# First layer: rotations from their angles, chunk matrices from four lags, another order of scans, factors and attention; 448 bytes of gap in the second feed-forward part

## The chip, the cores and the metric

The kernel runs on one core of one Trainium2 chip. The metric is the device time of one execution in microseconds, taken as the median of several runs. The engines are named as in the profile: PE (matrix products; PEld is its weight load), DVE (vector), ACT (activation functions), POOL (GpSimd) and SP, whose queue issues most of the DMAs.

## What is computed

Two blocks on a sequence of 256 tokens of width 1024, all in float32. The first block has two layers; the second block is a mixer, an attention on a memory and a mixture of 32 experts. The change is almost wholly in the first half of the first layer, which is this (cut):

```python
hn = rmsnorm(x, even_norm)
q, k, v, u = split(hn @ even_w_in)             # 512, 128, 128, 512 wide
o_attn = swa_sink_attention(rmsnorm(q), rmsnorm(k), v, sinks)   # 8 heads, window 128
# s5: 32 groups of 16 channels, 64 complex states each
lam = exp(a_re*dt) * (cos(a_im*dt) + i sin(a_im*dt))
w = (lam - 1) / a                              # complex
bu = einsum(u, w * b)
h[t] = lam * h[t-1] + bu[t]                    # scan over 256 steps
y = gelu(re(h) @ c_re - im(h) @ c_im + d * u)
o_ssm = y * sigmoid(y @ w_glu + b_glu)
x = x + concat(o_attn, o_ssm) @ even_w_out
x = x + (silu(rmsnorm(x) @ w_gate) * (rmsnorm(x) @ w_up)) @ w_down
```

The second layer has stick-breaking attention in place of the mixer above, and a feed-forward part of the same shape as the first one.

## The kernel before

The stages run one after the other: `even` (the first half of the first layer), `ffn` 0, `odd`, `ffn` 1, `mixer`, `mem`, `moe`. Weights come in 1 MB pieces through SP's queue. Each engine's instructions are put in order ahead of time from the program's order: an instruction takes its turn by its place in the program, and one whose inputs are not there yet lets later ones go ahead. `self.after(ins)` holds the instructions of its block behind `ins` where they are on the same engine. At run time each engine keeps the order that came out.

`even` (L379) does the state space part and the windowed attention beside each other.

- **Start.** The input, the parameters of the state space part, and the weights of `u` are loaded. `load_b` (L1817) loads the matrices b in eight DMAs of 32 KB through POOL's queue, in runs of 64 bytes; `load_rest` (L1825) loads d and c through SP's. `zeros` (L1804) clears `Q`, the two `bd` tiles and `KT`.
- **`scalars`** (L1859) makes, for 16 columns at a time, the powers of lam (`lam`), the factors `w` and `pw[0..4]` (lam to the i times w) and, by repeated squaring (`square`, L1855), the rotations `E[0..5]` of 4, 8, ... steps.
- **`factors`** (L1984) transposes c on PE. **`inputs`** (L1937) writes b times powers of lam into the `bd` tiles on DVE; **`inputs_T`** (L1945) transposes them on PE into `F`; **`shuffle`** (L2037) brings `u` into the order of four steps a column, on PE, as `U` and `Ud`.
- **`rotations`** (L1957) doubles a table `T` of 64 cosines and sines for each of 16 columns, from the `E`, in six steps of three DVE operations. **`decays`** (L1977) makes the magnitudes `D0`.
- The three products for q, k and v (`qkv`, two halves each) follow on PE; before the fourth half stands `states_in(0)`, whose result `v` the first scan reads.
- **`scan(j)`** (L2061), j from 0 to 3, is seven DVE operations: turn by `T`, two scans, turn back. **`outputs`** (L2003), held behind scan 0, writes c times `pw[i]` into `Q` on DVE for i from 0 to 4. **`direct`** (L2020) makes from `bd` and `Q` the matrices `KT` that act inside four steps: 128 small products on PE in four PSUM tiles, and 16 copies by ACT. **`reads(j)`** (L2085) are the products that give y.
- **Attention.** `qk_norm` (L555) norms k on DVE and transposes q and k on PE. `swa` (L590) goes through `soft_exp` (L618): scores on PE, mask and maximum on DVE, exponentials on ACT; then `transpose_p` (L658) and the product with v (`swo`).
- The order in the program is: rotations, decays, scan 0, outputs, direct, reads 0, qk_norm, the scores and exponentials of both halves, scan 1, reads 1, the rest of the attention, scans and reads 2 and 3, `gate` (L2100: gelu, the gate's product `glu`), and `out_proj`, whose products `acc` with `mixa` (attention) and `mixb` (state space) end the part.

In `ffn` (L268) a loop over 11 column pieces does 96 products `gu` and then 24 products `acc` for the piece before. `gap` puts unused bytes ahead of the pool of `s`, `hh` and `hl`: 448 in the first one and 320 in the second.

Of the kernel before, what the change touches and what calls it, by code (L numbers as in the profile page):

```python
# [17 lines left out]
P = 128  # L18
# [26 lines left out]
class K:  # L45
# [215 lines left out]
    def ffn(self, x, i):  # L261
# [117 lines left out]
    def even(self, x):  # L379
# [35 lines left out]
        V.tensor_copy(gc, pg[:, 0:8])  # L415
        s5.load_b()
        tu.append(self.load_cols(w, 1024))
# [38 lines left out]
        for j in range(3):  # L456
            pq = self.pa("qkv")
            wt = self.load_cols(w, j * 256)
            for t in range(2):
                if 2 * j + t == 3:  # L460

                    s5.states_in(0)
                    first = self.lastmm
                for k in range(8):
                    with self.after(*([first] if 2 * j + t >= 3 else [])):
                        self.mm(pq[:, t * 256:(t + 1) * 256], xT[:, k, t * P:(t + 1) * P], wt[:, k], k == 0, k == 7)
# [36 lines left out]
        for j in range(2, 4):  # L503
            wt = h().bitcast(F32).rearrange("p (a b) -> p a b", a=2)
            nc.sync.dma_start(wt, wo[j * 256:(j + 1) * 256, :].rearrange("(k p) n -> p k n", p=P))
            wos.append(wt)
        s5.reads(0)
# [5 lines left out]
        nc.gpsimd.memset(kT, 0.0)  # L513
# [43 lines left out]
    def qk_norm(self, pool, qk, qg, qT, kT, rq):  # L557
# [12 lines left out]
        for t in range(2):  # L570
# [3 lines left out]
        nc.vector.tensor_copy(rq.rearrange("p t (g h) -> p t g h", g=2),  # L574
                              r[:, :, 0:8].rearrange("p t (h g) -> p t g h", g=2))
# [14 lines left out]
    def swa(self, pool, t, qT, kT, v, sink8, rq, mix):  # L590
# [5 lines left out]
        def score(o, h):  # L596
            self.mm(o, qT[:, h // 2, ts], kT[:, h // 4, h % 2, 0:nk], True, True)

        att, den = self.soft_exp(pool, self.r8("att"), 8, nk, score, lambda h: self.band[:, 256 - nk:], 0.125,
                                 sink8, rq)  # L600
        yield
        pT = self.transpose_p(pool, self.r8("attT"), att, den, 8, nk)
# [12 lines left out]
    def soft_exp(self, pool, s, nh, nk, score, bias, scale, sink8, rq=None):  # L615
# [31 lines left out]
        for h in range(nh):  # L647
            nc.scalar.activation(s[:, h], src[h], AF.Exp, bias=nm[:, h:h + 1], scale=sc[h],
                                 accum_out=den[:, h:h + 1])
# [1134 lines left out]
class S5:  # L1784
# [19 lines left out]
    def zeros(self):  # L1804
        k, G = self.k, self.nc.gpsimd
        self.T = self.fp.tile([P, 2, 16, 64], F32, name="T")
        self.Q = self.fp.tile([P, 2, 16, 5, 32], F32, name="Q")
        G.memset(self.Q.rearrange("p c s k q -> p (c s k q)"), 0.0)
# [7 lines left out]
    def load_b(self):  # L1816
        nc, a = self.nc, self.k.a  # L1817
        self.bn = self.r0[:, 1024:1536].rearrange("p (c s q) -> p c s q", c=2, s=16)
        for c, n in enumerate(("ssm_b_im", "ssm_b_re")):
            for j in range(4):  # L1820
                nc.gpsimd.dma_start(self.bn[:, c, 4 * j:4 * j + 4],
                                    bass.AP(tensor=a[n].tensor, offset=a[n].offset + 2048 * j,
                                            ap=[[16, P], [8192, 4], [1, 16]]))
# [30 lines left out]

    def square(self, out, y):  # L1855
        self.cmul(out, y, y, 2)
        self.nc.vector.tensor_scalar(out[:, 2], out[:, 0], -1.0, None, op0=OP.mult)

    def scalars(self):  # L1859
# [33 lines left out]
        V.scalar_tensor_tensor(lam[1][:, 2:4], e[:, 0:2], -1.0, mb, op0=OP.mult, op1=OP.mult)  # L1893

# [17 lines left out]
        self.cmul(lam[2], lam[1], lam[1], 3)  # L1912
        self.cmul(lam[3], lam[1], lam[2], 3)
        self.mag4 = sm("mag4")
        V.tensor_tensor(self.mag4, mag, mag, op=OP.mult)
        V.tensor_tensor(self.mag4, self.mag4, self.mag4, op=OP.mult)
        e2 = cx("e2")
        self.E = [cx(f"E{i}") for i in range(6)]
        self.square(e2, e)
        self.square(self.E[0], e2)  # L1920
        for i in range(5):
            self.square(self.E[i + 1], self.E[i])
# [34 lines left out]
    def rotations(self, steps):  # L1957

        nc, k, sp = self.nc, self.k, self.sp
        V = nc.vector  # L1960
        T = self.T
        if 0 in steps:
            V.memset(T[:, 0, :, 0:1], 0.0)
            V.memset(T[:, 1, :, 0:1], 1.0)
            self.tb = k.r8("tb").rearrange("p (i m) -> p i m", i=2)
        tb = self.tb
        for i in steps:
            n = 1 << i
            shp = [P, 2, 16, n]
            t1, t2 = [tb[:, i, 0:32 * n].rearrange("p (c s a) -> p c s a", c=2, s=16) for i in range(2)]  # L1970
            V.tensor_tensor(t1, T[:, 1:2, :, 0:n].to_broadcast(shp),
                            self.E[i][:, 0:2, :, None].to_broadcast(shp), op=OP.mult)
            V.tensor_tensor(t2, T[:, 0:1, :, 0:n].to_broadcast(shp),
                            self.E[i][:, 1:3, :, None].to_broadcast(shp), op=OP.mult)
            V.tensor_tensor(T[:, :, :, n:2 * n], t1, t2, op=OP.add)

# [26 lines left out]
    def outputs(self):  # L2003
# [6 lines left out]
        for i in range(5):  # L2010
# [4 lines left out]
            for g in range(2):  # L2015
                pr = slice(64 * g, 64 * g + 64)
                qs = slice(16 * g, 16 * g + 16)
                V.tensor_tensor(Q[pr, :, :, i, qs], v1[pr], v2[pr], op=OP.add)

    def direct(self):  # L2020

        nc, k, Q, KT = self.nc, self.k, self.Q, self.KT
# [142 lines left out]
```

## Time and profile before

| | us |
|---|---|
| median of 3 runs (lowest, highest) | 1346.37 (1346.29, 1349.23) |
| the profiled execution, whole | 1346.77 |
| its span, first to last instruction | 1345.1 |
| PE busy in the span | 1230.3 |
| DVE busy in the span | 647.6 |
| ACT busy in the span | 485.6 |
| POOL busy in the span | 48.3 |

The page's shares are means over stages that have different limits. `even` is the first tenth of the span, so the page's slices tell little of it; the views that do are the chain of waits, the timeline and the table by stretches, each read for that stretch alone.

### The profile page before, as it was taken

The numbers are of one execution on the slowest core, as the hardware profiler recorded it, in microseconds if no ns is written. First come the engines' busy times: TensorE is split into PE (matmuls) and PEld (weight loads), VectorE is DVE, ScalarE is ACT, GpSimd is POOL, SyncE is SP. The second block draws the span as 40 slices with busy tenths as digits, with TensorE's granted clock in tenths as the row PEclk, the third lists the DMA queues.
The fourth block names the chain that finished last, engine by engine and source line by source line (L and its number), as shares of the span: only waits on it lengthen the run. The fifth ranks groups of instructions, "written<-read, shape, count | busy, mean of one in ns | idle before, by whom it ended". The sixth has DMA issues, their size and how long they took to land.

```text
span 1345.1 us, 20184 instructions
## 1 busy us (share of the span) xinstructions
PE 1230.3 (91%) x8427; PEld 909.6 (68%) x8427; DVE 647.6 (48%) x1137; ACT 485.6 (36%) x784; POOL 48.3 (4%) x72
## 2 busy tenths in 40 slices
PE   8899999999999999999999999999778777887786
PEld 7776899998998999998999998964122212222111
DVE  9955866666589766666777587431000101000001
ACT  3264644444577644444556555440000000000002
POOL 4010000001000000000300000000000000000000
PEclk9989999999999999999999999999989999889988
DMA  9401965644434865533562758789999999999996
GB/s 259 115 7 47 350 197 197 197 136 130 141 126 157 288 223 190 191 129 125 169 191 92 251 202 299 287 325 421 421 421 421 421 421 421 421 421 421 421 390 239
DMA packets 143436, 345.79 MB, mean 257 GB/s; under 512 B 9863, under 2 KB 100063, under 8 KB 120302
## 3 DMA queue, kind: packets, MB, share of 16 engines
q1 hardware_dynamic: 141418, 339.40, 68.4%
q0 software_dynamic: 1888, 5.06, 1.3%
q8 instruction: 67, 1.10, 0.3%
q14 instruction: 27, 0.22, 0.0%
q10 hardware_dynamic: 36, 0.01, 0.0%
HBM read 343.38 MB, written 1.06 MB: 256 GB/s over the span
## 4 chain that ended last, share of the span: by engine, by line
PE 58%; DMA 29%; DVE 8%; ACT 3%; issue 1%; SPq 0%; DVEq 0%; ACTq 0%
PE gu L77 20%; PE acc L77 15%; DMA w<-in_w_exp_down_dram 10%; DMA w<-in_w_exp_up_dram 8%; DMA w<-in_w_exp_gate_dram 7%; PE z L77 4%; PE qk L77 2%; PE y L77 2%; PE v L77 2%; PE prj L77 2%; PE mqk L77 2%; DMA b<-in_w_exp_gate_dram 1%; DMA b<-in_w_exp_up_dram 1%; DVE wh L182 1%; PE psT L1718 1%
## 5 line engine op out<-in xcount | busy, mean ns | idle before, releaser
L182 DVE TENSOR_TENSOR wh<-w,wh 128x1024 fp32r<-128x1024 f32 x229 | 276.1, 1223 | 133.0 <-ACT wh L181 132.2
L181 ACT ACTIVATE wh<-w 128x1024 fp32r<-128x1024 f32 x229 | 237.0, 1055 | 188.0 <-PE gu L77 64.7
L77 PE MATMUL gu<-fxh,wh 128*128 128x256 f32 x1408 | 246.9, 278 | 0.7 <-ACT fxh L181 0.7
L77 PE MATMUL gu<-w,xe 128*32 128x512 f32 x920 | 175.9, 663 | 52.3 <-DMA w<-in_w_exp_gate_dram 28.3
L77 PEld LDWEIGHTS gu<-fxh,wh 128*128 128x128 f32 x1408 | 214.5, 188 | 1.8 <-ACT fxh L181 0.9
L77 PE MATMUL gu<-fxl,wh 128*128 128x256 f32 x704 | 195.4, 278 | 0.0
L77 PEld LDWEIGHTS gu<-w,xe 128*32 128x32 f32 x920 | 39.1, 119 | 169.6 <-issue 66.5
L77 PEld LDWEIGHTS gu<-fxl,wh 128*128 128x128 f32 x704 | 133.0, 189 | 0.9
L77 PE MATMUL y<-w,hT 128*32 128x512 f32 x456 | 103.4, 612 | 18.6 <-DMA w<-in_w_exp_down_dram 13.1
L77 PE MATMUL acc<-wh,hh 128*128 128x512 f32 x352 | 110.1, 394 | 0.0
L77 PEld LDWEIGHTS y<-w,hT 128*32 128x32 f32 x456 | 24.5, 110 | 89.7 <-DMA w<-in_w_exp_down_dram 41.7
L77 PEld LDWEIGHTS acc<-wh,hh 128*128 128x128 f32 x352 | 64.4, 188 | 13.4
L77 PE MATMUL acc<-wh,hl 128*128 128x512 f32 x176 | 69.5, 395 | 0.0
L1417 DVE COPY ot<-owT 128x256 f32<-128x256 f32 x8 | 3.4, 428 | 135.7 <-PE owT L1415 135.7
L1459 DVE TENSOR_TENSOR y<-y,gu 128x512 f32<-128x512 f32 x8 | 8.1, 1016 | 113.2 <-PE gu L77 103.4
L1456 ACT ACTIVATE y<-gu 128x512 f32<-128x512 f32 x8 | 4.8, 598 | 149.2 <-PE gu L77 149.2
L1490 DVE COPY y<-y 128x512 f32<-128x512 f32 x7 | 4.8, 692 | 106.1 <-PE y L77 106.1
L1476 ACT ACTIVATE hT<-hT 128x512 f32<-128x512 f32 x8 | 4.8, 597 | 139.5 <-PE hT L1474 139.5
L77 PE MATMUL qk<-oxh,wh 128*128 128x256 f32 x256 | 48.7, 285 | 0.0
L1488 ACT ACTIVATE y<-y 128x512 f32<-128x512 f32 x9 | 5.4, 597 | 114.8 <-PE y L77 114.8
L77 PE MATMUL z<-mxh,wh 128*128 128x256 f32 x256 | 46.6, 281 | 0.0
L77 PE MATMUL gu<-b,xe 128*32 128x512 f32 x104 | 34.7, 611 | 7.1 <-DMA b<-in_w_exp_gate_dram 4.2
(539 smaller groups left out, 2046.1 us busy)
## 6 DMA issues: line engine op xcount, KB each, us to landing
w<-in_w_exp_gate_dram SPq DMA_DIRECT2D x57, 1024.0 KB, 19.8
w<-in_w_exp_up_dram SPq DMA_DIRECT2D x54, 1024.0 KB, 19.8
w<-in_w_exp_down_dram SPq DMA_DIRECT2D x51, 1024.0 KB, 19.8
w<-in_ffn_w_gate_dram SPq DMA_DIRECT2D x22, 1024.0 KB, 5.5
w<-in_ffn_w_up_dram SPq DMA_DIRECT2D x22, 1024.0 KB, 6.8
w<-in_ffn_w_down_dram SPq DMA_DIRECT2D x22, 1024.0 KB, 4.9
w<-in_w_in_dram SPq DMA_DIRECT2D x20, 1024.0 KB, 6.0
w<-in_odd_w_in_dram SPq DMA_DIRECT2D x12, 1024.0 KB, 6.2
```

What stands on the lines that cost most here:

```text
L77: self.lastmm = self.nc.tensor.matmul(out, lhsT, rhs, start=start, stop=stop, **kw).ins
L181: return (self.nc.scalar.activation(h, src, AF.Copy).ins, (eng or self.nc.vector).tensor_tensor(l, src, h.bitcast(F32), op=OP.subtract).ins)
L182: (eng or self.nc.vector).tensor_tensor(l, src, h.bitcast(F32), op=OP.subtract).ins)
L1417: V.tensor_copy(ot, ps[:, 0:256].rearrange("p (t n) -> p t n", t=2))
L1456: nc.scalar.activation(s, hs[0], AF.Silu)
L1459: V.tensor_tensor(sk, s.rearrange(turn, k=4), hs[1].rearrange(turn, k=4), op=OP.mult)
L1476: nc.scalar.activation(hT, ps.rearrange("p (f n) -> p f n", f=4), AF.Copy)
L1488: nc.scalar.activation(y[:, h], yps[h], AF.Copy)
L1490: V.tensor_copy(y[:, h], yps[h])
L1718: k.turned = k.nc.tensor.transpose(ps[:, i * P:(i + 1) * P], xg[:, t, (4 * c + i) * P:(4 * c + i + 1) * P], k.ident).ins
```

## The change

In `even` and its helpers:

- `load_b` issues its eight DMAs from SP, behind the 1 MB piece of `u`'s weights and ahead of `load_rest`.
- `scalars` ends with `lam` and `mag4`. The factors `w` and `pw` go into a new function `holds`, called behind scan 0 and ahead of `outputs`. The repeated squares are gone.
- `rotations` makes the whole table at once: the angle times 4, 8, ... from a constant row, a reduction to one turn in six DVE operations on 1024 columns, and sine and cosine by ACT.
- `inputs_T` stands ahead of `shuffle`; rotations and decays stand right behind it. `states_in(0)` stands before the third half of the q, k, v products in place of the fourth.
- `direct` makes each of its 16 blocks once (32 products, one PSUM tile) and copies it to four places.
- Behind `outputs` come: qk_norm (its DVE part behind the last `Q`), scan 1 (behind the norm), the scores and exponentials, direct, reads 0, scan 2, reads 1, the rest of the attention (its ACT part behind the last exponential), scan 3, reads 2 and 3. The first half's scores use the tile of the turned input in place of one of the four work tiles. The gelus stand behind the last exponential. `kT` is cleared by ACT, where POOL did it.

In the second `ffn` the gap is 448 bytes.

```diff
-            self.gap((448, 320)[i], ctx)
+            self.gap(448, ctx)
...
+        tu.append(self.load_cols(w, 1024))
         s5.load_b()
-        tu.append(self.load_cols(w, 1024))
         s5.load_rest()
...
+        s5.inputs_T()
         s5.shuffle(uT)
-        s5.inputs_T()
+        s5.rotations()
+        s5.decays()
...
-                if 2 * j + t == 3:
+                if 2 * j + t == 2:
                     s5.states_in(0)
...
-        s5.rotations(range(6))
-        s5.decays()
         s5.scan(0)
         with self.after(s5.last):
+            s5.holds()
             s5.outputs()
-        s5.direct()
...
-        s5.reads(0)
...
-        self.qk_norm(ap, qk, qg[:, 0], qT, kT, rq)
+        with self.after(s5.lastq):
+            self.qk_norm(ap, qk, qg[:, 0], qT, kT, rq)
+        with self.after(self.normed):
+            s5.scan(1)
...
         next(swa[0])
         next(swa[1])
-        for j in range(1, 4):
-            s5.scan(j)
+        scored = self.lastmm
+        s5.direct()
...
+        with self.after(scored):
+            s5.reads(0)
+        s5.scan(2)
+        s5.reads(1)
+        with self.after(self.exped):
+            for part in swa:
+                next(part, None)
+        s5.scan(3)
+        for j in range(2, 4):
             s5.reads(j)
-            if j == 1:
-                for part in swa:
-                    next(part, None)
...
-                nc.gpsimd.dma_start(self.bn[:, c, 4 * j:4 * j + 4],
+                nc.sync.dma_start(self.bn[:, c, 4 * j:4 * j + 4],
...
+        V.tensor_tensor(g, self.th[:, :, None].to_broadcast([P, 16, 64]),
+                        self.four[:, None].to_broadcast([P, 16, 64]), op=OP.mult)
+        V.tensor_scalar(n, g, 1.0 / (2.0 * math.pi), magic, op0=OP.mult, op1=OP.add)
+        V.tensor_scalar(n, n, -magic, None, op0=OP.add)
+        for t in (TWO_PI_1, TWO_PI_2, TWO_PI_3):
+            V.scalar_tensor_tensor(g, n, -t, g, op0=OP.mult, op1=OP.add)
+        V.tensor_scalar(g, g, 3.141592, -3.141592, op0=OP.min, op1=OP.max)
+        nc.scalar.activation(self.T[:, 0], g, AF.Sin)
+        nc.scalar.activation(n, g, AF.Abs)
+        nc.scalar.activation(self.T[:, 1], n, AF.Sin, bias=self.quarter, scale=-1.0)
...
+            for c in range(2):
+                for g in range(4):
+                    s = 4 * g + i
+                    k.mm(pk[32 * g:32 * g + 32, i], self.bd[c][:, s, 3], Q[:, c, s, 0:4, :], c == 0, c == 1,
+                         tile_position=(0, 32 * g))
```

## Rows read from the trace of the kernel before

**Rows 1.** Chain that ended last, first 140 us; columns start, us, what:
```profile
44.80 1.75 PE v L77 x16
46.57 1.24 DVE abgh L2072
...
64.16 9.96 PE s5K L77 x144
...
91.90 4.78 ACT att L648 x16
...
97.21 1.98 PE swo L77 x4
```

**Rows 2.** Stretches: us, busy of PE PEld DVE ACT POOL, PEclk, DMA share, GB/s:
```profile
7.68:46.57 38.89, 35.00 (x210) 29.06 (x209) 35.16 (x136) 13.16 (x30) 6.99 (x11) 1.00 0.78 214
97.21:101.00 3.79, 3.79 (x13) 2.00 (x14) 3.79 (x4) 3.07 (x5) 0.00 (x0) 0.55 0.02 4
97.21:133.62 36.41, 36.41 (x172) 22.50 (x173) 21.50 (x31) 16.75 (x24) 0.58 (x1) 0.95 0.14 44
```

**Rows 3.** DVE's groups by shape, 7.4 to 46.6 us (busy, mean ns):
```profile
L1975 DVE TENSOR_TENSOR T<-tb 128x1024 f32<-128x1024 f32 x1 | 1.2, 1224 | 0.0
L1981 DVE COPY D<-mag 128x1024 f32<-128x1024 f32 x1 | 0.7, 680 | 0.0
L1853 DVE TENSOR_TENSOR pw<-cm,cm 128x48 f32<-128x48 f32 x4 | 0.8, 202 | 0.0
```

**Rows 4.** Timeline to 60 us (start, us, engine, line; in brackets idle before, releaser):
```profile
10.20 4.72 SPq L1834 DMA_DIRECT2D params<-in_ssm_c_im_dram  x2
13.88 0.68 DVE L1981 COPY D<-mag 128x1024 f32<-128x1024 f32 x1
18.05 0.42 ACT L1941 ACTIVATE wh<-params 64x256 f32<-64x256 f32 x1 [1.09 <-DMA params<-in_ssm_b_re_dram]
25.95 5.34 PE L77 MATMUL qkv<-w,ex 128*128 128x256 f32 x24
33.66 1.93 PE L77 MATMUL U<-uT,ident 128*32 128x256 f32 x32 [2.36 <-DVE uT L449]
35.52 4.09 PE L1953 MATMUL s5F<-ident,wh 128*128 128x128 f32 x32
50.95 1.06 ACT L566 ACTIVATE qT<-qk 128x1024 f32<-128x1024 f32 x1
51.75 0.68 DVE L2011 TENSOR_TENSOR ub<-cd,w 128x512 f32<-128x512 f32 x1
```

**Rows 5.** Timeline, 65 to 97 us, around the norm and the exponentials:
```profile
65.45 1.39 DVE L2018 TENSOR_TENSOR Q<-ub 64x512 f32<-64x512 f32 x2
...
69.39 0.17 DVE L574 COPY rq<-qr 128x16 f32<-128x16 f32 x1
...
77.30 0.66 PE L77 MATMUL kT<-ident,qk 128*64 128x128 f32 x8
...
80.36 0.29 DVE L633 CUSTOM_DVE_ANT_0 att<-sc,band 128x128 f32<-128x128 f32 x1 [10.59 <-PE sc L77]
...
82.79 0.49 ACT L648 ACTIVATE att<-att,nm,rqs 128x128 f32<-128x128 f32 x1 [1.35 <-DVE nm L645]
```

**Rows 6.** ACT's groups by shape, 82 to 97.3 us:
```profile
L648 ACT ACTIVATE att<-att,nm,rqs 128x256 f32<-128x256 f32 x8 | 4.7, 586 | 0.5 <-DVE att L665 0.5
L648 ACT ACTIVATE att<-att,nm,rqs 128x128 f32<-128x128 f32 x8 | 3.8, 480 | 1.4 <-DVE nm L645 1.4
```

**Rows 7.** Table by stretches, single pieces of the first and second feed-forward part:
```profile
161.10:178.00 16.90, 16.90 (x122) 15.84 (x122) 11.96 (x18) 9.86 (x16) 0.00 (x0) 1.00 0.87 298
178.00:194.40 16.40, 16.40 (x123) 15.42 (x122) 10.17 (x12) 7.59 (x11) 0.00 (x0) 1.00 0.58 193
481.09:497.58 16.49, 16.49 (x122) 15.41 (x122) 10.17 (x12) 7.59 (x11) 0.00 (x0) 1.00 0.73 246
497.58:514.49 16.91, 16.91 (x122) 15.82 (x122) 10.17 (x12) 7.59 (x11) 0.00 (x0) 1.00 0.58 187
```

More of the change, by code (lines that the diff above doesn't have):

```diff
@@ L464, in even @@
                 for k in range(8):
-                    with self.after(*([first] if 2 * j + t >= 3 else [])):
+                    with self.after(*([first] if 2 * j + t >= 2 else [])):
                         self.mm(pq[:, t * 256:(t + 1) * 256], xT[:, k, t * P:(t + 1) * P], wt[:, k], k == 0, k == 7)
@@ L527, in even @@
         next(swa[1])
-        for j in range(1, 4):
-            s5.scan(j)
+        scored = self.lastmm
+        s5.direct()
+        for j in range(2, 4):
+            wt = h().bitcast(F32).rearrange("p (a b) -> p a b", a=2)
+            nc.sync.dma_start(wt, wo[j * 256:(j + 1) * 256, :].rearrange("(k p) n -> p k n", p=P))
+            wos.append(wt)
+        with self.after(scored):
[6 more added lines that the diff above has]
+        s5.scan(3)
+        for j in range(2, 4):
             s5.reads(j)
-            if j == 1:
-                for part in swa:
-                    next(part, None)
         fctx.close()
@@ L1807, in zeros @@
         self.Q = self.fp.tile([P, 2, 16, 5, 32], F32, name="Q")
+        self.four = self.fp.tile([P, 64], F32, name="four")
+        G.iota(self.four, pattern=[[4, 64]], base=0, channel_multiplier=0, allow_small_or_imprecise_dtypes=True)
+        self.quarter = self.fp.tile([P, 1], F32, name="quarter")
+        self.nc.vector.memset(self.quarter, math.pi / 2)
         G.memset(self.Q.rearrange("p c s k q -> p (c s k q)"), 0.0)
@@ L1893, in scalars, with holds @@
         V.scalar_tensor_tensor(lam[1][:, 2:4], e[:, 0:2], -1.0, mb, op0=OP.mult, op1=OP.mult)
+        self.cmul(lam[2], lam[1], lam[1], 3)
+        self.cmul(lam[3], lam[1], lam[2], 3)
+        self.mag4 = sm("mag4")
+        V.tensor_tensor(self.mag4, mag, mag, op=OP.mult)
+        V.tensor_tensor(self.mag4, self.mag4, self.mag4, op=OP.mult)
+        self.th, self.pr3 = th, pr3
+    def holds(self):
+        V, sm, cx = self.nc.vector, self.sm, self.cx
+        lam, pr3 = self.lam, self.pr3
         den, t1, t2, t3 = sm("den"), cx("t1", 2), cx("t2", 2), cx("t3")
@@ L1911, in scalars @@
             self.cmul(self.pw[i + 1], lam[1], self.pw[i], 3)
[L1912 to L1922, printed above, removed]
     def inputs(self):
@@ L1955, in inputs_T, with rotations @@
                 nc.scalar.activation(F[:, c, 4 * j:4 * j + 4], ps.rearrange("p (t n) -> p t n", t=4), AF.Copy)
-    def rotations(self, steps):
-        nc, k, sp = self.nc, self.k, self.sp
+    def rotations(self):
+        nc, k = self.nc, self.k
         V = nc.vector
[L1961 to L1975, printed above, removed]
+        tb = k.r8("tb").rearrange("p (i s a) -> p i s a", i=2, s=16)
+        g, n = tb[:, 0], tb[:, 1]
+        magic = 12582912.0
+        V.tensor_tensor(g, self.th[:, :, None].to_broadcast([P, 16, 64]),
[8 more added lines that the diff above has]
+        nc.scalar.activation(self.T[:, 1], n, AF.Sin, bias=self.quarter, scale=-1.0)
     def decays(self):
@@ L2017, in outputs @@
                 qs = slice(16 * g, 16 * g + 16)
[L2018 removed]
+                self.lastq = V.tensor_tensor(Q[pr, :, :, i, qs], v1[pr], v2[pr], op=OP.add).ins
     def direct(self):
         nc, k, Q, KT = self.nc, self.k, self.Q, self.KT
[L2023 to L2032 removed]
+        ps = k.ps("s5K")
+        pk = ps.rearrange("p (s b q) -> p s b q", s=4, b=4)
+        for i in range(4):
+            for c in range(2):
[3 more added lines that the diff above has]
+                         tile_position=(0, 32 * g))
+        for g in range(4):
             for b in range(4):
[L2034 to L2035 removed]
+                nc.scalar.activation(KT[32 * b:32 * b + 32, 4 * g:4 * g + 4, b:4], pk[32 * g:32 * g + 32, :, 0:4 - b],
+                                     AF.Copy)
     def shuffle(self, uT):
@@ L2105, in gate @@
         yg = self.work().rearrange("p (j t a) -> p j t a", j=4, t=4)
-        for i in range(2):
-            nc.scalar.activation(yg[:, 2 * i:2 * i + 2], self.ys[i], AF.Gelu_apprx_tanh)
+        with k.after(k.exped):
+            for i in range(2):
+                nc.scalar.activation(yg[:, 2 * i:2 * i + 2], self.ys[i], AF.Gelu_apprx_tanh)
         yt = [k.ps("yt"), k.ps("yt")]
```

40 lines of the change are left out of this document (11 added, 29 removed).

## The prediction

> **What bounds the kernel now.** I read the page first, to see which engine is busy where, and then left its means aside: the change lies in the first 140 of 1345 us. There I read the chain of waits from its end backwards, and at each change of engine the timeline beside it. The reader should see four links.
>
> (a) Scan 0 starts at 46.57, when PE delivers its input v [rows 1]. v itself waits behind 48 instructions of q, k, v products (24 of them at 25.95, as many right ahead of v) and behind U and s5F, of which U started only when DVE had uT [rows 1, 4]. DVE is busy 35.16 of the 38.89 us up to there, so it is the engine that made uT and the T late [rows 2]. (b) Behind scan 0 DVE makes Q, and the s5K products on PE wait for it until 64.16, hold PE for 10 us, and k's transposes and the scores stand behind them: DVE sat 10.59 us before the first scores at 80.36, although the norm was done at 69.39 [rows 1, 5]. (c) The exponentials start at 82.79 and end at 91.90 + 4.78 = 96.68 [rows 1, 5]. Their own work is 8 times 0.48 and 8 times 0.586, 8.5 us [rows 6]; the other 5.3 us ACT spent behind a copy of turned probabilities that stands ahead of the second eight in its order and itself waits for DVE [rows 1, 6]. (d) From 97.21 PE has no hole until the products with mixb, 36.41 of 36.41 us [rows 2]. From there on the rest of the kernel hangs on this PE time, so what moves 97.21 moves the end by as much.
>
> **The change part by part, up to scan 0.** DVE loses the 23 steps of holds, the 28 steps of the squares, and the 18 of the doubling. The small steps take 0.2 us each by themselves, and about half of that where the next one doesn't wait for them [rows 3]; I take 0.15 for holds and 0.125 for the squares, which interleave with large operations: 3.5 and 3.5 us (bounds 2.3 to 4.6 and 2.8 to 5.6). The doubling has three operations each of 1024 columns (1.224 us) and of 512, 256, 128, 64, 32 columns; by halves above a floor of 0.2 they make 9.2 us. Added are seven operations on 1024 columns. The product with the angle and the three combined ones I put at the row of T, 1.22; the three with a constant lie between that and the copy of D0, 0.68 [rows 3], and I take the copy, the nearest in form: 4.9 + 2.0 = 6.9 us (bounds 4.8, all seven at the copy's price, to 8.6). In sum DVE has 9.3 us less to do (bounds 5.7 to 14.6), and its 35.16 busy us from 7.68 on [rows 2] would, without a wait, end at 42.8 before and 33.5 now; T's last DVE step, with some 1.5 of waits, near 35. ACT's sine, absolute value and sine follow, three passes of 1024 columns at 1.06 [rows 4], so T is there near 38, 41.6 at the worst bound. No row shows a sine of 1024 columns; a pass of the same columns is the nearest.
>
> PE then decides. From 25.95 it has 32 instructions of q, k, v (5.34/24 each: 7.1), s5F (4.1), U (1.9), v (1.75), 14.9 us in any order [rows 1, 4]; the order of inputs_T and shuffle costs nothing as both must come before v. With a few tenths for the R product that gives v at 41.2 and scan 0 at 41.3, 5.3 us ahead. Of that, 3.5 come from the 16 q, k, v instructions that now stand behind v, and the rest from the wait for uT, 2.36. Bounds: 39.5 if u's products end sooner, 43.5 if PE waits for bd or c once more.
>
> The b matrices now go through SP. They landed at 18.05 from POOL [rows 4], and POOL's clearing of Q no longer stands ahead of their issue. But SP's queue has its own waits: its issue of c already took 4.72 us for two pieces while it waited for earlier loads [rows 4], and now eight pieces stand ahead of d, c and the q, k, v weights. I take b at 16.5 to 18 and c some 2 to 3 us later. Later c is covered by u's second half, which PE can do first; if PE's order puts c's transposes ahead, u and all behind slips by up to 2 us, which is the upper bound above. The Trainium skill ("DMA: Bandwidth & Descriptors", Issuing engines are not separate DMA queues) speaks against this edit: DMAs from any engine share the same 16 DMA engines, and another issuer saves only issue time. By that b would land at 18 as before; the sum would not gain from it, and the start of scan 0 would move by nothing, since PE decides it.
>
> **From scan 0 to the exponentials.** Scan 0 took 5.2 (46.57 to 51.75) [rows 1, 4]: end 46.5. holds, now exposed on DVE: 3.5, to 50. Q five times, each two products of 0.68 that overlap to 1.2 and a pair of 1.39 [rows 4, 5], 2.65: 13.3, to 63.3. The norm, all behind it: a reduction of 1024 columns 1.2, one of 256 0.4, eighteen small steps 3.6, the copy 0.17: 5.4, normed at 68.7 against 69.56. So the attention gains little up to here; holds and the norm in one line have eaten the 5.3. Scan 1 stands next on DVE, 5.2, to 73.9. Meanwhile PE makes k's transposes and the scores, which took 3.1 from the first transpose at 77.30 to the first mask at 80.36 [rows 5]: there by 71.8, behind scan 1. Scores to exponentials took 82.79 - 80.36 = 2.4 [rows 5]: exponentials start at 76.3, 6.5 ahead. What is removed here is s5K's 10 us on the path: the new direct has a quarter of the products (2.5 us on PE, ready when Q's fourth step is done near 60.7) and lies in PE's hole; its 16 copies of some 0.43 lie in ACT's, before 76.3. Were that cover gone, they would cost up to 2.5 + 6.8.
>
> With the attention's ACT part behind the last exponential, the sixteen run without a hole: 8.5 + 0.2, end at 85.0 against 96.68. Two copies of 0.6 and swo starts at 86.9 against 97.21: **10.3 us**. Scan 2 and 3 on DVE (10.4, next to 3.8 of normalisation, from 79 on) end by 95, and PE has swo, transposes, reads 2 and the products with mixa until then. So PE's 36.4 us run through again, and the end of the part moves by 10.3. Bounds: 5 (scan 0 at 43.5, DVE's order letting scan 2 in between the scores, holds at 4.6) to 14 (scan 0 at 39.5; and swo not at half clock: the granted clock from 97.21 to 101 was 0.55, mostly the lower level, 1.2 of 2.4 GHz, so these 3.8 us would shrink by some 1.7 [rows 2] if PE is at the upper level by then).
>
> The clearing of kT on ACT (about 1 us early, ACT idle) and the tile for the first scores cost nothing.
>
> **The gap.** Pieces of the two feed-forward parts have the same instructions, the same busy times of the other engines and a granted clock of 1.00, but take 16.40 in the first (gap 448) from its third piece on, and by turns 16.91 and 16.49 in the second (gap 320): from 464 to 615 us five and four of them. The first one's second piece took 16.90 too [rows 7]. So the pace has at least two values, not from the clock, and the gap is the only difference in the code. If 448 brings the second part to what the first one shows, four pieces gain 0.51 and four 0.09: **2.4 us**. If the pace hangs on something else, it is 0, or a loss of 1.7 when the four of 16.49 take 16.91 too. I take 2.4, by the row that has the same gap.
>
> **Sum.** 1346.77 (the profiled execution, 0.4 above the median) - 10.3 - 2.4 = 1334.1; against the median 1333.7.
>
> **Rivals.**
> A. The gap does nothing; the pace is set elsewhere. For it: a piece at 16.90 under gap 448 [rows 7]. Time 1346.4 - 10.3 = 1336.1.
> B. Half the gain: long operations of the new rotations fill each small pause on DVE between the steps that lead to lam, so that bd comes late, PE waits, and scan 0 starts at 44; and scan 2 slips in ahead of the second half's scores. The D0 copy, late in the program, stood at 13.88 as such a filler [rows 4]. 1346.4 - 5 - (0 to 2.4) = 1339.0 to 1341.4.
> C. Slower: T comes last. In the program rotations stand behind inputs, uT and shuffle. If b lands at 28 because its 64-byte runs and the waits of SP's queue hold it up, inputs (8.7 us) end at 37, uT and Ud at 41, and the 6.9 to 8.6 follow without overlap, to 49; the three ACT passes fall among F's eight copies, and T is there at 55 to 57. Everything behind scan 0 is 45.6 us long as above, so the change loses from a scan 0 at 51.6 on, 1 us for each us: at 57 it is 1351.8. Against it: b landed at 18 by the slower way, and T's angles need only the first steps of scalars, so nothing but order keeps T from starting.
> D. The pace tips in the first feed-forward part, as its second value shows up under gap 448 too [rows 7]: eight pieces by 0.51, 4.1 lost: 1337.8.
>
> **Chances.** Forecast 0.42, A 0.28, B 0.16, C 0.05, D 0.09. A measurement of this kernel tells 0.3%, 4 us, from no change: faster means below 1342.3. Forecast, A, D and most of B lie there, with their spreads: 0.86; same 0.10 (the rest of B, D's far end, the milder half of C); slower 0.04. The range leaves 2 in 10 out: from 1329 (14 in place of 10.3, 2.4, and a pace that tips the good way for a piece or two) to 1341 (B).
>
> **What would show it.** Scan 0's first operation near 41; T's second sine before 40; the last Q near 63 and the norm's copy near 69; the first exponential near 76 and sixteen without a hole; swo near 87, and no hole in PE from there; pieces of 16.40 in the second feed-forward part. Wrong it would be if scan 0 stays at 46, if ACT's copies of KT stand among the exponentials, or if PE shows holes behind 87.

## The result, and the profile after

The changed kernel takes 1332.92 us (median of 4 runs, 1331.50 to 1335.14). The kernel before, run beside it, took 1347.53 us (4 runs, 1346.29 to 1349.23). The ratio is 0.9892, with a 95% interval from 0.9873 to 0.9912: 14.6 us faster, 11.9 to 17.1 by the interval. The forecast was 1333.7 us in a range from 1329 to 1341. The profiled execution took 1333.31 us with a span of 1331.6, 13.5 us less than the span of before.

The chain that ended last, in the changed kernel (start us, us, what), beside [rows 1]:

```profile
31.21 6.67 PE qkv L77 x30
37.88 1.75 PE v L77 x16
39.72 1.24 DVE abgh L2081
...
66.18 1.12 PE kT L77 x8
...
83.10 4.79 ACT att L658 x16
...
89.05 1.08 PE swo L77 x4
```

s5K, 10 us of the chain in [rows 1], is gone from it. Between scan 0 and k's transposes the whole chain is DVE's (scan 0, holds, Q, then the norm), where before it changed to PE.

The table by stretches of the changed kernel (us, busy us and count of PE, PEld, DVE, ACT, POOL, then granted clock, DMA share, GB/s), beside [rows 2] and [rows 7]:

```profile
7.64:39.72 32.08, 32.04 (x201) 26.98 (x200) 25.01 (x75) 16.37 (x33) 0.00 (x0) 1.00 0.83 236
66.18:75.75 9.57, 9.57 (x53) 8.16 (x54) 9.18 (x40) 6.94 (x18) 0.00 (x0) 0.72 0.00 1
89.05:120.36 31.31, 31.31 (x147) 18.29 (x147) 16.19 (x23) 16.37 (x24) 0.57 (x1) 1.00 0.15 51
136.54:149.42 12.88, 12.88 (x100) 12.83 (x99) 10.71 (x17) 8.92 (x10) 0.00 (x0) 0.87 1.06 364
485.79:502.19 16.40, 16.40 (x122) 15.41 (x122) 10.17 (x12) 7.59 (x11) 0.00 (x0) 1.00 0.60 193
502.19:518.59 16.40, 16.40 (x122) 15.41 (x122) 10.17 (x12) 7.59 (x11) 0.00 (x0) 1.00 0.58 193
```

Up to scan 0, PE is now busy 32.04 of 32.08 us and DVE 25.01: the two have changed places as the limit. The last two lines are pieces of the second feed-forward part at one pace.

The timeline of the changed kernel (start, us, engine, line; in brackets idle before, releaser), beside [rows 4] and [rows 5]:

```profile
14.04 0.84 ACT L1952 ACTIVATE wh<-params 64x256 f32<-64x256 f32 x2 [0.66 <-DMA params<-in_ssm_b_im_dram]
15.78 0.84 ACT L1952 ACTIVATE wh<-params 64x256 f32<-64x256 f32 x2 [0.90 <-DMA params<-in_ssm_b_re_dram]
...
19.76 0.63 PE L2000 MATMUL s5C<-ident,params 128*128 128x128 f32 x4
...
38.15 1.15 ACT L1984 ACTIVATE T<-tb,quarter 128x1024 f32<-128x1024 f32 x1
...
58.57 1.96 PE L77 MATMUL s5K<-Q,wh 128*32 128x128 f32 x64 [1.18 <-DVE Q L2027]
...
66.15 0.17 DVE L583 COPY rq<-qr 128x16 f32<-128x16 f32 x1
...
77.01 1.22 DVE L2081 TENSOR_TENSOR abgh<-v,T 128x1024 f32<-128x1024 f32 x1
...
79.74 0.17 DVE L655 TENSOR_SCALAR nm<-m 128x8 f32<-128x8 f32 x1
...
82.28 0.78 DVE L675 TENSOR_TENSOR att<-att,den 128x512 f32<-128x512 f32 x1
...
83.10 0.60 ACT L658 ACTIVATE att<-att,nm,rqs 128x256 f32<-128x256 f32 x1 [2.75 <-DVE att L675]
```

The milestones side by side (starts in us of the span unless it says end; the forecast's last four are before less the moves that it summed):

| | before | forecast | after | moved by |
|---|---|---|---|---|
| scan 0 | 46.57 | 41.3 | 39.72 | 6.85 |
| last Q, end | 66.84 | 63.3 | 61.2 | 5.6 |
| norm's copy | 69.39 | 68.5 | 66.15 | 3.2 |
| first exponential | 82.79 | 76.3 | 74.07 | 8.7 |
| last exponential, end | 96.68 | 85.0 | 87.89 | 8.8 |
| swo | 97.21 | 86.9 | 89.05 | 8.2 |
| products with mixb | 133.62 | 123.3 | 120.36 | 13.3 |
| second piece of the first feed-forward part | 161.10 | 150.8 | 149.42 | 11.7 |
| eleventh piece of the second one | 614.69 | 602.0 | 600.59 | 14.1 |
| end of span | 1345.1 | 1332.4 | 1331.6 | 13.5 |

Few rows moved as planned. Up to the first exponential each came earlier than forecast (scan 0 by 1.6 us, the last Q by 2.1, the first exponential by 2.2); the last exponential's end came 2.9 later and swo 2.1 later; the products with mixb came 2.9 earlier. The next two sections are about these, the gap, and which edit brought what.

### The profile page after: what moved, and what is told of

The parts are those of the page before. It is cut to its first block, busy times and chain, and to the rows that moved or that the text cites. A ratio compares the mean times of both kernels' runs of the same rounds, so it can differ in the third digit from the quotient of the medians.

```text
span 1331.6 us, 19755 instructions
## 1 busy us (share of the span) xinstructions
PE 1221.8 (92%) x8235; PEld 902.4 (68%) x8235; DVE 640.7 (48%) x1097; ACT 489.4 (37%) x788; POOL 40.6 (3%) x64
## 3 DMA queue, kind: packets, MB, share of 16 engines
HBM read 343.38 MB, written 1.06 MB: 259 GB/s over the span
## 4 chain that ended last, share of the span: by engine, by line
PE 59%; DMA 30%; DVE 6%; ACT 4%; issue 1%; SPq 0%; DVEq 0%; ACTq 0%
PE gu L77 20%; PE acc L77 14%; DMA w<-in_w_exp_gate_dram 9%; DMA w<-in_w_exp_down_dram 9%; DMA w<-in_w_exp_up_dram 7%; PE z L77 4%; PE qk L77 2%; PE v L77 2%; PE prj L77 2%; PE mqk L77 2%; PE y L77 1%; DMA b<-in_w_exp_up_dram 1%; DMA b<-in_w_exp_gate_dram 1%; DVE wh L182 1%; PE u L77 1%; PE psT L1728 1%
## 5 line engine op out<-in xcount | busy, mean ns | idle before, releaser
L77 PE MATMUL gu<-b,xe 128*32 128x512 f32 x104 | 41.1, 732 | 7.0 <-DMA b<-in_w_exp_gate_dram 4.2
L77 PE MATMUL z<-mxh,wh 128*128 128x256 f32 x256 | 46.6, 281 | 0.0
```

Source lines behind the costliest of these rows:

```text
L77: self.lastmm = self.nc.tensor.matmul(out, lhsT, rhs, start=start, stop=stop, **kw).ins
```

## Experiments

| kernel | median us | before beside it | ratio, 95% interval | span profiled |
|---|---|---|---|---|
| changed kernel | 1332.92 | 1347.53 | 0.9892 (0.9873, 0.9912) | 1331.6 |
| e1, gap 320 in the second part | 1336.58 | 1348.23 | 0.9916 (0.9898, 0.9933) | 1333.5 |
| e2, gaps swapped | 1334.40 | 1348.23 | 0.9903 (0.9882, 0.9925) | 1332.0 |
| e3, den twice | 1331.89 | 1348.23 | 0.9877 (0.9861, 0.9894) | 1330.1 |
| e4, norm early | 1333.64 | 1348.23 | 0.9881 (0.9863, 0.9899) | 1332.3 |
| u1, old direct | 1332.60 | 1349.06 | 0.9874 (0.9858, 0.9891) | 1330.8 |
| u2, v ahead of the fourth half | 1339.10 | 1349.06 | 0.9925 (0.9908, 0.9941) | 1337.0 |
| u3, b from POOL | 1335.56 | 1348.44 | 0.9897 (0.9881, 0.9914) | 1336.9 |
| b1, before with den twice | 1346.05 | 1348.44 | 0.9989 (0.9977, 1.0001) | 1343.3 |
| b2, before with the rotations | 1353.64 | 1348.44 | 1.0042 (1.0025, 1.0059) | 1350.3 |
| b3, before with v early | 1345.65 | 1348.44 | 0.9973 (0.9963, 0.9983) | 1344.8 |
| c1, den twice, holds early | 1328.72 | 1349.06 | 0.9850 (0.9834, 0.9867) | 1325.3 |
| c2, and outputs early | 1326.78 | 1349.06 | 0.9842 (0.9823, 0.9861) | 1323.8 |

Kernels timed on different chips are compared by their ratios (0.1% is 1.35 us), and a step inside a kernel by its trace: the intervals are some 2.5 us wide to either side, so steps of 2 us are read from the traces. By the ratios alone, e1 to e4, u1 and u3 are not told apart from the changed kernel, u2 is slower than it (by 0.0033, where the two intervals' half-widths combine to 0.0025), and c1 and c2 are faster.

### The gap: e1 and e2

```diff
-            self.gap(448, ctx)
+            self.gap((448, 320)[i], ctx)      # e1
+            self.gap((320, 448)[i], ctx)      # e2
```

> The changed kernel with the second feed-forward part's gap back at 320 bytes; every engine's order is the same. Theory: the gap alone sets the pace of that part's pieces, so they alternate again between 16.91 and 16.49 us where the changed kernel has 16.40, and the ten pieces' starts from the second to the eleventh span 150.5 us in place of 148.1: the kernel loses 2.4 us. Rival: the pace comes from what ran earlier (the first layer's new order, or where in time the part starts), then the pieces stay at 16.40 and nothing is lost.

> The changed kernel with 320 bytes of gap in the first feed-forward part and 448 in the second. Theory that the gap sets the pace: the first part's pieces now alternate between 16.91 and 16.49 us (150.5 us between the starts of its second and its eleventh piece, 148.1 in the changed kernel), the second part stays at 16.40; loss 2.4 us. Rival, that the first part is quick by itself and only the second one feels the gap: no loss.

Stretches of single pieces, of the second part in e1:

```profile
485.70:502.19 16.49, 16.49 (x122) 15.41 (x122) 10.17 (x12) 7.59 (x11) 0.00 (x0) 1.00 0.56 192
502.19:519.10 16.91, 16.91 (x122) 15.82 (x122) 10.17 (x12) 7.59 (x11) 0.00 (x0) 1.00 0.56 187
```

and of the first part in e2:

```profile
181.13:197.62 16.49, 16.49 (x123) 15.41 (x122) 10.17 (x12) 7.59 (x11) 0.00 (x0) 1.00 0.60 192
197.62:214.53 16.91, 16.91 (x123) 15.82 (x122) 10.17 (x12) 7.59 (x11) 0.00 (x0) 1.00 0.57 187
```

Wherever the gap is 320, pieces alternate between 16.49 and 16.91 at a granted clock of 1.00; wherever it is 448, they take 16.40 from the third piece on (the second one took 16.90 in the changed kernel, 452.49 to 469.39, and 16.40 in others with the same gap; no run here shows why). From the second to the eleventh piece that is 150.10 us in e1's second part (452.29 to 602.39) and in e2's first part (147.72 to 297.82), against 148.10 in the changed kernel (452.49 to 600.59) and 150.51 in the kernel before (464.18 to 614.69). The difference is 2.0 where the alternation begins with a quick piece and 2.4 where it begins with a slow one. The rival, that the pace comes from what ran earlier, falls: e2 moved it into a part whose code and past were untouched. Why 128 bytes of address do this, no run here shows.

### The second eight exponentials: e3 and b1

```diff
-        den = pool.tile([P, nh], F32, tag="den", name="den")
+        den = pool.tile([P, nh], F32, tag=f"den{nk}", name="den")
```

> The changed kernel with a tile of its own for the sums (den) of each half of the windowed attention. Theory: the second eight exponentials wait because they write the den that the first half's two normalising products (the second ends at 83.06) still read; without that they start when their bias is there, near 80, and end near 84.8 in place of 87.9. The time gains little, 0 to 0.6 us, because TensorE has no idle time from 66.18 on but 0.59 us ahead of the first product with v at 89.05. Rival, the prediction's reading: they wait behind a copy of turned probabilities that stands ahead of them on ACT; then they still start after 83. Second rival: the exponentials bound the part; then the time falls by about 3 us.

> The kernel before with a tile of its own for the sums (den) of each half of the windowed attention. Theory: there too the second eight exponentials waited, until 91.90, for the first half's normalising products that read the same den; they start near 88.6 when their bias is there, end near 93.3 in place of 96.7, and as TensorE stood idle ahead of the product with v at 97.21, that one comes about 3 us earlier: gain 2 to 3 us. Rival: the copy of turned probabilities ahead of them in ACT's order holds them; then nothing moves (under 0.5 us).

The first of the second eight, on ACT's timeline, in e3:

```profile
80.03 0.60 ACT L658 ACTIVATE att<-att,nm,rqs 128x256 f32<-128x256 f32 x1 [1.84 <-DVE nm L655]
```

and in b1:

```profile
89.39 0.60 ACT L648 ACTIVATE att<-att,nm,rqs 128x256 f32<-128x256 f32 x1 [1.85 <-DVE nm L645]
```

In both kernels the releaser changes from the normalising product (DVE att) to the bias nm, and the exponentials start 3.1 and 2.5 us earlier (in b1 although its scan 0 came 0.9 late in this execution). So what ended the wait was den: the exponentials write the sums that the other half's normalisation still read. The copy of turned probabilities, which the prediction named, was not it: in the changed kernel no copy stands ahead of the second eight in ACT's order, and they wait all the same. (In the kernel before one does, from 90.76 to 91.36, and in b1 it stands behind them, so b1 by itself does not part the two; e3 does.)

Den is not the whole hole. In e3 ACT still idles 1.84 us for the bias nm. DVE makes it late, since its order has four operations of scan 2 among the small steps that lead from the second half's masks to nm: from 77.01 to 79.74 in the changed kernel. In the first half, with nothing between, nm starts 0.5 us behind the last mask (73.34 to 73.86). No run took scan 2 out of there.

In time, e3 gives 1.0 us at swo (88.00 for 89.05) and its ratio is not told apart from the changed kernel's; b1 gives 1.5 us by its ratio, with an interval that reaches just over 1. As expected of e3, PE had almost no idle time to give back by then.

### The chunk matrices: u1

The whole of `direct` (and its 16 copies) is that of the kernel before, in the new order.

```diff
-        ps = k.ps("s5K")
+        for s4 in range(4):
+            ps = k.ps("s5K")
...
+                for b in range(4):
+                    for c in range(2):
+                        k.mm(pk[32 * b:32 * b + 32, i, b:4], self.bd[c][:, s, 3], Q[:, c, s, 0:4 - b, :],
+                             c == 0, c == 1, tile_position=(0, 32 * b))
```

> The changed kernel with the old direct: 128 products in four PSUM tiles where the changed one makes each block once with 32. Theory: in the new order the products lie in the time from 58.6 to 66.2 in which TensorE waits for the norm; about three quarters of them stand ahead of k's transposes and take some 6 us, the rest lies among the scores. So the transposes still start near 66 and the kernel loses 0 to 2 us. Rival, the prediction's ledger: the products were 10 us on the path and their removal is the larger part of the gain; then this version loses 5 us or more.

PE's timeline in u1:

```profile
58.28 3.65 PE L77 MATMUL s5K<-Q,wh 128*32 128x128 f32 x128 [1.17 <-DVE Q L2027]
62.12 2.73 PE L77 MATMUL s5K<-Q,wh 128*32 128x128 f32 x66 [0.19 <-ACT KT L2045]
65.79 0.66 PE L77 MATMUL kT<-ident,qk 128*64 128x128 f32 x8 [0.94 <-DVE qk L582]
```

and a stretch of u1, k's transposes and the scores:

```profile
65.79:74.28 8.49, 8.49 (x71) 6.33 (x71) 8.24 (x36) 4.84 (x13) 0.00 (x0) 1.00 0.01 3
```

Four times the products cost nothing that can be told from the changed kernel: scan 0 at 39.44, the transposes at 65.79 (66.18), swo at 88.22 (89.05). They run while PE would wait for the norm. There is also a return for them. The changed kernel's PE idles 5.65 us ahead of k's transposes and then runs them and the scores at a granted clock of 0.72 (66.18 to 75.75 above), much of it at the lower level of 1.2 GHz: the eight transposes take 1.12 us. In u1 PE has been busy 6.29 of the 8.79 us before, the granted clock is 1.00, and the same eight take 0.66.

### What makes scan 0 early: b2, b3 and u2

```diff
 # b2, on the kernel before: rotations, scalars, holds and zeros of the changed kernel, and
-        s5.rotations(range(6))
+        s5.rotations()
...
         with self.after(s5.last):
+            s5.holds()
             s5.outputs()
 # b3, on the kernel before
-                if 2 * j + t == 3:
+                if 2 * j + t == 2:
 # u2, on the changed kernel
-                if 2 * j + t == 2:
+                if 2 * j + t == 3:
```

> The kernel before with only the new rotations, the repeated squares gone and holds behind scan 0; every order else as before. Theory: VectorE is done with uT some 2.4 us earlier, so v and scan 0 come near 44.2 in place of 46.57, but holds now stand behind scan 0 with 2.1 us, so that Q and all behind it move by less than 0.7 us and so does the time. Rival: the rotations carry a good part of the gain; then the time falls by 2.5 us or more.

> The kernel before with only the product that gives v put ahead of the third half of the q, k, v products in place of the fourth. Theory: TensorE could deliver v 3.5 us earlier, near 43, but VectorE's line ahead of scan 0 ends near 44.1, so scan 0 starts near 44.3 and the kernel gains 2 to 2.5 us. Rival: the DVE line has slack, then 3.5 us; second rival: the s5K products and the wait for the norm hide it, then under 1 us.

> The changed kernel with the product that gives v back ahead of the fourth half of the q, k, v products. Theory: scan 0 waits for v, the 16 instructions put ahead of it take 3.5 us, and from scan 0 to the norm VectorE has no idle time, so scan 0 starts near 43.2 in place of 39.72, k's transposes near 69.7 in place of 66.18, and the kernel loses 3 to 3.5 us. Rival: the rotations T (their last pass ended at 39.3) or the q and k that the norm needs decide, and the loss is under 1 us.

In b2 (PE's and DVE's timeline):

```profile
17.67 0.63 PE L1991 MATMUL s5C<-ident,params 128*128 128x128 f32 x4 [1.76 <-DMA params<-in_ssm_c_re_dram]
...
33.82 2.84 PE L1955 MATMUL s5F<-ident,wh 128*128 128x128 f32 x24 [1.60 <-DVE Ud L2051]
36.50 8.37 PE L77 MATMUL qkv<-w,ex 128*128 128x256 f32 x38
44.70 1.90 PE L77 MATMUL v<-U,F 128*128 128x64 f32 x16
46.70 1.23 DVE L2072 TENSOR_TENSOR abgh<-v,T 128x1024 f32<-128x1024 f32 x1 [7.36 <-PE v L77]
```

in b3 (DVE's):

```profile
43.38 1.23 DVE L1975 TENSOR_TENSOR T<-tb 128x1024 f32<-128x1024 f32 x1
44.71 1.22 DVE L2072 TENSOR_TENSOR abgh<-v,T 128x1024 f32<-128x1024 f32 x1
```

and in u2 (DVE's and PE's, then two stretches):

```profile
42.71 1.23 DVE L2081 TENSOR_TENSOR abgh<-v,T 128x1024 f32<-128x1024 f32 x1 [6.90 <-PE v L77]
69.15 1.12 PE L77 MATMUL kT<-ident,qk 128*64 128x128 f32 x8 [3.96 <-DVE qk L582]
90.00:95.00 5.00, 3.10 (x18) 1.86 (x18) 2.52 (x4) 4.95 (x13) 1.04 (x2) 0.93 0.12 5
95.00:100.00 5.00, 5.00 (x26) 3.38 (x27) 4.90 (x9) 3.28 (x6) 0.58 (x1) 0.73 0.03 6
```

Scan 0 waits for two things, T and v. With T early alone (b2), DVE idles 7.36 us for v, which still has 48 instructions of q, k, v ahead of it, 38 of them in one row; and holds, now behind scan 0, push Q and the norm back by 2.7 us (its copy at 72.05). The kernel gets slower by 5.7 us (3.4 to 8.0 by the interval), where 0 was expected: the earlier uT (29.2 for 33.6) was used up by PE's own order. With v early alone (b3), scan 0 starts right behind T's last step at 44.71, 1.9 us earlier, and the kernel gains 3.6 us (2.3 to 5.0).

T early and v early do not make up the 6.85 us by themselves. b2 and u2 both have T early and v last, and scan 0 stands at 46.70 in the one and 42.71 in the other: the 4.0 us between them belong to the edits that u2 has besides, the loads of b through SP and inputs_T ahead of shuffle with the order behind it. The traces show where they lie. In b2 PE waits 1.76 us for c, so that the product R behind u's last one starts at 26.00 where u2 has 24.00, and then 0.52 us for uT and 1.60 inside s5F; u2 has none of these waits. No run makes one of these edits without the other on the kernel before. In the changed kernel the two things that scan 0 needs come almost together, T at 39.30 and v at 39.61; in e1 to e4 the profile names T as the later one, with scan 0 at 39.22 to 40.06.

Undone from the changed kernel (u2), v last costs 3.0 us at scan 0 and at k's transposes, as expected, but 5.4 in the span and 4.4 by the ratios: the late exponentials now leave PE idle ahead of swo (3.10 busy of 5 us from 90), and it goes on at a granted clock of 0.73. Here PE's idle time is paid for twice, as the wait itself and in the lower clock behind it.

### The loads of b: u3

```diff
-                nc.sync.dma_start(self.bn[:, c, 4 * j:4 * j + 4],
+                nc.gpsimd.dma_start(self.bn[:, c, 4 * j:4 * j + 4],
```

> The changed kernel with the eight loads of b back on POOL's queue. Theory: TensorE's products decide when v comes, the loads' issuer is hidden; scan 0 stays within 0.5 us of 39.72 and the time within 0.7 us. Rival: b lands 1 us or more later, the bd tiles and s5F move with it, and the kernel loses as much.

DVE's, ACT's and PE's timeline in u3:

```profile
16.55 0.84 ACT L1952 ACTIVATE wh<-params 64x256 f32<-64x256 f32 x2 [2.02 <-DMA params<-in_ssm_b_im_dram]
17.95 0.69 DVE L1945 TENSOR_TENSOR ub<-params,l 128x512 f32<-128x512 f32 x1
18.54 0.63 PE L2000 MATMUL s5C<-ident,params 128*128 128x128 f32 x4 [1.69 <-DMA params<-in_ssm_c_re_dram]
19.98 0.84 ACT L1952 ACTIVATE wh<-params 64x256 f32<-64x256 f32 x2
35.05 0.17 DVE L504 TENSOR_SCALAR sink<-sink 128x8 f32<-128x8 f32 x1 [3.84 <-DMA sink<-in_sinks_dram]
44.27 1.15 ACT L1984 ACTIVATE T<-tb,quarter 128x1024 f32<-128x1024 f32 x1
45.45 1.23 DVE L2081 TENSOR_TENSOR abgh<-v,T 128x1024 f32<-128x1024 f32 x1 [3.25 <-ACT T L1984]
```

From SP, ACT waited for the two halves of b until 14.04 and 15.78. From POOL it waited for the first until 16.55; the second was there by 17.95 at the latest, when DVE read it (ACT's 19.98 is only its turn, with no wait ahead). Yet POOL's issues ended at 12.34 and SP's at 14.14. The Trainium skill ("DMA: Bandwidth & Descriptors", Issuing engines are not separate DMA queues) says that another issuer saves only the time of issuing. These rows, of one execution each, differ from that: the later issue landed earlier, by 2.5 us and by at most 2.2.

The expectation missed: scan 0 stands at 45.45, not within 0.5 us of 39.72. One part of this is PE's. Its order in u3 has c's products behind 28 of u's where the changed kernel has them behind 44, and it waits 1.69 us for c there (18.54 above; no wait at 19.76 in the changed kernel), besides 0.89 for u's weights at 9.35. So v ends at 41.92 in place of 39.61. The other kernels agree: R, behind u's last product, starts at 24.95 to 26.79 in the five kernels with b from POOL and at 23.89 to 24.65 in the nine with b from SP. The loads' issuer was not hidden: it moves v. The rest is T's. With b's loads elsewhere, DVE's order changed: two small steps on the attention's sinks now stand behind the first of T's steps, ahead of all others, and the 8 numbers that they need land at 35.05. T then comes last, which is the mechanism of the prediction's rival C, through another DMA than the one named there. By the ratios u3 loses 0.7 us, not told apart from nothing; this profiled execution was the slowest of its four (1338.56 us, the others 1334.08 to 1335.83). So what the issuer is worth in the whole time stays open, and so does how late the sinks land in other executions; that it moves v, and that the order makes T hang on the sinks, is shown. In the changed kernel the same two steps stand at 35.12, ahead of T's last step.

### The norm earlier, and two versions that are faster: e4, c1, c2

```diff
 # e4: the norm ahead of the outputs, scan 1 behind both
+        with self.after(s5.last):
             self.qk_norm(ap, qk, qg[:, 0], qT, kT, rq)
+            s5.outputs()
 # c1: den twice; holds behind T's last step on DVE (turned)
-        with self.after(s5.last):
+        with self.after(s5.turned):
             s5.holds()
+        with self.after(s5.last):
             s5.outputs()
 # c2: den twice; holds and outputs behind T's last step on DVE
-        with self.after(s5.last):
+        with self.after(s5.turned):
             s5.holds()
             s5.outputs()
```

> The changed kernel with the norm of q and k placed ahead of the outputs in the program, so that its small steps lie among the operations that make Q, and scan 1 behind both. Theory: TensorE's only large idle time in this part is the 8 us from 57 to 66.18, where it waits for the norm, and from there on it bounds the part; the norm's last step comes near 63 in place of 66.3, and the kernel gains 2 to 3 us. Rival: the end of the attention is set by DVE's whole work, which stays the same, so that scan 1 and the masks end as before and the time doesn't move (within 0.5 us).

> The changed kernel with den twice as in e3_den_twice, and with holds held behind the last step of T's reduction in place of scan 0, so that its 2.1 us lie in the 3.6 us in which VectorE waits for v ahead of scan 0. Theory: VectorE's line from scan 0 to the norm sets when k's transposes start; they start near 64 in place of 66.18 and the kernel gains 2 us on e3_den_twice, 3 us on the changed kernel. Rival: TensorE's products and ACT's copies of KT ahead of them take the gain back (under 0.7 us on e3_den_twice).

> As c1_holds_early, with the outputs too held behind T's last step alone: holds and the first fifth of Q stand ahead of scan 0. Theory: VectorE has no idle time left from T to the norm; scan 0 starts about 1.3 us later than in the changed kernel, near 41, and the norm 3.3 us earlier, so k's transposes start near 63; gain 3 us on e3_den_twice, 4 us on the changed kernel. Rival: scan 0's delay passes on to the reads, and it is no better than c1_holds_early.

k's transposes in e4, on PE's timeline:

```profile
65.32 1.11 PE L77 MATMUL kT<-ident,qk 128*64 128x128 f32 x8 [2.87 <-DVE qk L582]
```

and scan 0, k's transposes and swo in c2, on DVE's and PE's:

```profile
39.24 1.21 DVE L2081 TENSOR_TENSOR abgh<-v,T 128x1024 f32<-128x1024 f32 x1
61.66 0.66 PE L77 MATMUL kT<-ident,qk 128*64 128x128 f32 x8 [2.91 <-DVE qk L582]
82.05 1.08 PE L77 MATMUL swo<-att,v 128*64 128x512 f32 x4
```

e4 was a miss: 65.32 in place of the 63 expected, and no gain that can be told. The norm's small steps then take turns with Q's operations until 63.4 and go on by themselves behind them, so the line from scan 0 to the norm gets only 1.1 us shorter (25.5 us for 26.6). Taking work out of that line does help. DVE idled 3.64 us ahead of scan 0; with holds in there (c1) the transposes come at 63.08, with the first part of Q too (c2) at 61.66, and scan 0 is no later than in the changed kernel (39.24, where 41 was expected). swo moves from 89.05 to 82.05 and the span from 1331.6 to 1323.8. c2's interval (0.9823 to 0.9861) lies wholly below that of the changed kernel (0.9873 to 0.9912): it beats both kernels, the one before by 19 to 24 us. So does c1's (0.9834 to 0.9867); the two are not told apart from each other. That the line from scan 0 to the norm bounds this part is shown by u2, c1 and c2 together: moved by +3.0, -3.1 and -4.5 us at the transposes, their spans move by +5.4, -6.3 and -7.8 (den's share of some 1 us in the last two). Part of what c2 gains beyond that goes with PE's clock: k's transposes take 0.66 us there, 1.12 in the changed kernel and in u2.

## Why the prediction held, point by point

- **Scan 0.** Its sum of PE's work ahead of v was 14.9 us; from the first s5F product at 24.90 to v's end at 39.6 it is 14.7. What failed is the start: u's products ended 1.05 us earlier than in [rows 4], hence 39.72 for 41.3, inside its bound of 39.5. The waits for c, 0.36 and 0.74 us in the kernel before, are gone; by u3's rows this comes with b's loads on SP, which the prediction's sum counted as worth nothing. The doubling, summed as it says (halves above 0.2), gives 9.6 us and not 9.2, the trace has 9.1; nothing hangs on it. The prices of the rotations were right: 1.21 for the products, 0.69 for the steps with a constant, 1.06, 1.04 and 1.15 for ACT's passes, T there at 39.30 ("before 40", though later than the "near 38" of its sum). PE decides, but by 0.31 us only.
- **The order of inputs_T and shuffle "costs nothing".** b2 speaks against it: where U still stood ahead of s5F, PE waited 1.60 us inside s5F. In the changed kernel s5F fills the wait for uT. The term was right only because the change makes that swap.
- **From scan 0 to the norm.** 16.3 us for holds and Q against 16.8, 5.1 against 5.4 for the norm. It said that the attention would gain little up to there, and it gained 3.2.
- **s5K's 10 us "removed".** The price was read rightly from [rows 1], the cause only by half: the prediction gave a quarter of the products and their place in PE's hole. u1 has all the products back and loses nothing, so the new order alone takes them off the path, since scan 1 and the norm come ahead of what needs them.
- **The exponentials "run without a hole".** Wrong. From the first to the last they take 13.8 us as before, 13.9. The hole in [rows 6] had been put down to a copy in ACT's order, and the change reorders that. e3 shows that 3.1 us of it were den; the other 2 are the wait for the bias behind operations of scan 2. That is a milder form of one condition of rival B, that scan 2 slips in ahead of the second half's scores; its other one, scan 0 at 44, did not come. A releaser that writes nothing the waiting instruction reads was the hint for den: [rows 6] names DVE att as what ended the idle time, not a copy. From the last exponential to swo the sum took 1.9 us (85.0 to 86.9) where its own two copies of 0.6 make 1.2; the trace has 1.16. This slip hid part of the miss: the exponentials ended 2.9 late and swo came 2.1 late.
- **From swo to the end of the part "36.4 us run through again".** Also off, the other way. The stretch is 31.31 us. In [rows 2] the mean granted clock of that stretch was 0.95, now 1.00, which is 1.8 of it (36.41 by 0.05). About 3 more is the product y of reads that now lie ahead of swo: behind it the chain of before has two rows of them,

```profile
108.73 3.06 PE y L77 x26
...
112.70 2.18 PE y L77 x20
```

  that of after one,

```profile
96.63 2.40 PE y L77 x22
```

  The prediction counted reads 2 behind swo ("swo, transposes, reads 2"); as scan 2 came early, PE did them from 83.70 on, ahead of swo, and only reads 3 were left. The clock's share it had named, but in its bound alone. The two errors, 2.1 too much and 5.1 too little, are why the part gained 13.3 and not 10.3.
- **1.6 us given back at once.** The first piece of the first feed-forward part took 12.88 at a granted clock of 0.87. Before, the profile had

```profile
149.80:161.10 11.30, 11.30 (x100) 11.25 (x99) 10.72 (x17) 8.92 (x10) 0.00 (x0) 1.00 1.07 369
```

  This is not the change's: b3, with the order of before in that stretch, has

```profile
147.45:160.07 12.62, 12.62 (x100) 12.56 (x99) 10.54 (x16) 8.92 (x10) 0.00 (x0) 0.89 1.07 367
```

  and over all fourteen kernels the piece takes 11.28 to 12.88. The one execution of before on which the prediction rested was a lucky one there; the kernel before, timed beside the experiments, had medians of 1348.23 to 1349.06 where its first was 1346.37.
- **The gap.** 2.4 forecast, 2.41 measured (150.51 less 148.10), and shown to be the cause by e1 and e2. Rivals A and D are out. Rival C, T last by far, did not come in the changed kernel; u3 shows its mechanism.
- **The rest.** From the experts' first products to the end of the span it is 451.3 us before and 452.2 after; the other twelve kernels have 450.7 to 452.3. That 0.9 us is scatter.

So the number came out within 1 us partly by luck, because its errors cancel: swo's 2.1 and the first piece's 1.6 against the 5.1 of the stretch behind swo. What held as a mechanism is that scan 0 comes early, that DVE's line from there to the norm sets the attention's start, and the gap; the hole among the exponentials and the stretch behind swo were read wrongly.

## What to carry to other kernels

Before removing work from a path, ask whether another order would hide it: here four times the products cost nothing once something else was waited for. Where a stage waits for two inputs that come close together, moving one of them gains only as far as the other allows: v alone brought scan 0 1.9 us, T alone nothing, and the holds that moved with it a loss. A small tile shared by two halves of a stage (den, 8 numbers wide) can hold an engine for 3 us, and the releaser's name tells it.

## What the runs showed of the hardware that was not expected

- Where `s`, `hh` and `hl` start, 128 bytes apart, sets the pace of a run of matrix products: 16.40 us or 16.49 and 16.91 by turns for the same piece, at the same granted clock and the same busy times of the other engines.
- Products that nobody needed in that number kept PE's granted clock at 1.00 (u1), where idling 5.65 us cost the next ones nearly twice their time (1.12 for 0.66).
- In u3 a load of 8 numbers, issued at 24.50 behind loads of 1 MB, landed at 35.05 and held DVE for 3.84 us, because DVE's order put its use ahead of the rotations.
